# Output projection in two parts: w_out's block 3 and the second tile's channels move to the first part; the norms' factor -1/2 moves into a small step

## The chip, the core and the metric

The kernel runs on one core of a Trainium2 chip. The metric is the time of one execution in microseconds (us) of that core; three runs of the kernel before are summed up by their median. Beside them stands one profiled execution, from which every row below is taken. Engines: TensorE (PE, its weight loads PEld), VectorE (DVE), ScalarE (ACT), GpSimd (POOL), SyncE (SP, which here issues all the DMAs, in order).

## What is computed

A decoder block on 1024 tokens and 16 meta tokens of 1024 channels, in float32: a mixer of eight attention heads and a gated short convolution (512 channels each), an output projection, and an MLP with squared ReLU. The part that the change touches:

```python
def rms_norm(x, g):
    y = x * lax.rsqrt(jnp.mean(x * x, axis=-1, keepdims=True) + EPS)
    return y * g

y = concat([head_rms_norm(y_attn, ...), head_rms_norm(y_conv, ...)])   # 512 + 512 channels
h = h + y @ w_out                                                      # 1024 x 1024
hn = rms_norm(h, norm_mlp_g)
h = h + jnp.square(relu(hn @ w_ff1)) @ w_ff2
h = rms_norm(h, final_norm_g)
```

## The kernel before

**Precision.** Every large product is made of three matmuls on a high and a low part of each operand: `split` makes the high part by a cast on ScalarE and the low part by a subtraction on VectorE or, where it is told so, on POOL.

**Stages.** Projections, attention and the first part of the output projection share one long loop over (head, query tile), in which TensorE's spare time is filled from a generator (`fill`, a quota of us for each step): first with the projections, then with `out_conv`. `out_conv` (first part) multiplies the 512 convolution channels with blocks 4 to 7 of w_out (`wc`), for 8 tiles of 128 tokens and two halves of 512 columns, adds x and stores the rows in `h_scr`. The second part follows the loop: `mixed(i, ks)` multiplies tile `TOK[i]`'s attention channels (blocks 0 to 2 from `y_att`, block 3 from `y3`, which stays on the chip) with blocks `ks` of w_out (`wa`), `row_done(i)` adds the stored row, takes the norm (`rest_of`) with the gain `gmlp` to `hn`, and stores the row; `turn_rows(i)` transposes `hn` on TensorE in eight pieces, and several steps form the operands and their sums for the MLP (a form of Strassen's). TOK is 0, 4, 1, 5, 2, 3, 6, 7: the second tile is tile 4.

**Loads of the first part.** `wo_ahead` (line 612, at the end of the last q group) loads the first tile's convolution channels and blocks 4 to 7 whole into a pool of their own. `out_begin` (line 622, at the end of the last k group) frees the projections' memory, opens the pool `op` and splits these blocks. In `out_conv` each tile loads the next one's channels into one of two places `raw` of 512 columns; the tiles 1 to 3 also load blocks 0 to 2 through the same two places (`load_wo`), and tile 6 the attention channels of tile 0.

**Loads of the second part.** After the loop, lines 818 to 831, in this order: tile 4's channels, block 3 of w_out in two halves, two rows, the gain, the split of the channels, the split of block 3, the third tile's channels, the last row's store. The gain's DMA alone is not held in program order, nor are the two POOL multiplications by -1/2 behind it. Because block 3 comes last, the first two tiles run as follows:

```python
for i in range(2):
    mixed(i, range(NP - 1))        # blocks 0 to 2 of both tiles
for i in range(2):
    mixed(i, [NP - 1])             # block 3
    row_done(i)
    split_rows(i + 2)              # channels of a later tile, low part on POOL
    fetch_y(i + 3)
```

**Order.** A planner orders what is not held in program order (`pin` after the loop, `pe` inside it) by modelled times; each engine works its queue in order.

**The norm.** 1/sqrt is exp(-ln/2) with one Newton step. Before, the step gives -2 times the value (`minus_two_rstd`, and lines 844 to 846), and each gain is multiplied by -1/2 when it is loaded (`gain`, line 133): half on VectorE and half on POOL for the first norm, all on POOL for the two others.

Of the kernel before, what the change touches and what calls it, by code (L numbers as in the profile page):

```python
# [20 lines left out]
P = 128  # L21
# [20 lines left out]
def hymba_block(  # L42
# [53 lines left out]
    halfc = const.tile([P, 1], F32, name="halfc")  # L96
    nc.vector.memset(halfc, -0.5)
# [23 lines left out]
    def minus_two_rstd(ss, n, rows=P):  # L121
# [5 lines left out]
        pin(nc.vector.tensor_scalar(v, ss, 1.0 / n, EPS, op0=ALU.mult, op1=ALU.add))  # L127
        pin(nc.scalar.activation(r, r, AF.Exp, scale=-0.5))
        pin(nc.vector.scalar_tensor_tensor(out=t, in0=r, scalar=r, in1=v, op0=ALU.mult, op1=ALU.mult))
        pin(nc.vector.scalar_tensor_tensor(out=t, in0=t, scalar=-3.0, in1=r, op0=ALU.add, op1=ALU.mult))  # L130
        return t

    def gain(pool, src, tag, early=False):

        g = pool.tile([P, D], F32, name=tag, bufs=1)
        nc.sync.dma_start(g, src.broadcast_to([P, D]))
        for c in range(2):
            cs = slice(c * 512, (c + 1) * 512)
            if early and c == 0:
                nc.vector.tensor_scalar(g[:, cs], g[:, cs], -0.5, None, op0=ALU.mult)  # L140
            else:
                nc.gpsimd.tensor_tensor(out=g[:, cs], in0=g[:, cs], in1=halfc.broadcast_to([P, 512]), op=ALU.mult)
        return g
# [39 lines left out]
    gmix = gain(ep, norm_mix_g, "gmix", True)  # L183
# [26 lines left out]
    def norm(n):  # L210
# [4 lines left out]
        r = minus_two_rstd(ss, D, rows)  # L215
# [385 lines left out]
    def split_y(raw, n):  # L601
        yh = after["op"].tile([P, 4, P], F32R, name="yh", bufs=2)
        yl = after["op"].tile([P, 4, P], F32R, name="yl", bufs=2)
        split(yh[:, :n], yl[:, :n], raw, nc.gpsimd)
        return yh, yl
# [6 lines left out]
    def wo_ahead():  # L612
# [3 lines left out]
        raws = after["raws"] = [tw.tile([P, D], F32, name=f"ahead{k}") for k in range(NC)]  # L616
        y = after["y0"] = tw.tile([P, NC, P], F32, name="y0")
        nc.sync.dma_start(y, y_rows(y_conv, 0))
        for k in range(NC):
            nc.sync.dma_start(raws[k], wo[(NP + k) * P:(NP + k + 1) * P])  # L620

    def out_begin():
# [6 lines left out]
        after["wa"] = [[op.tile([P, D], F32R, name=f"wa{i}{k}") for i in range(2)] for k in range(NP - 1)]  # L629
# [3 lines left out]
        for k in range(NC):  # L633
            split(*w[k], after["raws"][k])
        after["wc"], after["y"] = w, y
# [7 lines left out]
    def out_conv():  # L643
# [4 lines left out]
        for t in range(NT):  # L648
# [4 lines left out]
            for c in range(2):  # L653
# [9 lines left out]
                if c == 0 and t + 1 < NT:  # L663
# [3 lines left out]
                elif c and 0 < t < NP:  # L667
# [129 lines left out]
    rows, ys_, yraw = {}, {0: after["y"][0]}, {}  # L797

    def fetch_y(i):
        if i < NT:  # L800
            if i == 1:
                raw = os.tile([P, (NP - 1) * P], F32, name="raw1")
            else:
                raw = after["op"].tile([P, 512], F32, name="raw", bufs=2)[:, :(NP - 1) * P]
# [3 lines left out]
    def split_rows(i):  # L808
        if i < NT:
            ys_[TOK[i]] = split_y(yraw.pop(i), NP - 1)  # L810
# [7 lines left out]
    fetch_y(1)  # L818
    w3 = [os.tile([P, D], F32R, name=f"wa{i}3") for i in range(2)]
    raw3 = [after["op"].tile([P, 512], F32, name="raw", bufs=2) for _ in range(2)]  # L820
    for c, raw in enumerate(raw3):
        dma(raw, wo[(NP - 1) * P:NP * P, c * 512:(c + 1) * 512])
    fetch_row(0)
    fetch_row(1)
    gmlp = gain(os, norm_mlp_g, "gbc")
    split_rows(1)
    for c, raw in enumerate(raw3):
        split(*(w[:, c * 512:(c + 1) * 512] for w in w3), raw)
    wa = after["wa"] + [w3]
    fetch_y(2)  # L830
    dma(*after["kept"])

    def rest_of(row, g, dst, gap=()):
# [10 lines left out]
        pin(nc.vector.tensor_scalar(v, ss, 1.0 / D, EPS, op0=ALU.mult, op1=ALU.add))  # L844
        pin(nc.vector.scalar_tensor_tensor(out=t, in0=r, scalar=r, in1=v, op0=ALU.mult, op1=ALU.mult))
        pin(nc.vector.scalar_tensor_tensor(out=t, in0=t, scalar=-3.0, in1=r, op0=ALU.add, op1=ALU.mult))
# [612 lines left out]
```

## Time and profile before

| | us |
|---|---|
| median of three runs | 1211.78 (1211.17 to 1214.83) |
| the profiled execution | 1215.61 |
| its span, first to last instruction | 1213.5 |
| TensorE busy in it | 1170.1 |
| VectorE, ScalarE, POOL busy | 729.2, 544.2, 225.8 |
| second part of the output projection, first matmul to the end of the last set | 514.4 to 580.5 |

The span is the profiled execution's own time less what lies around it; the median of the runs is 3.83 us less than the profiled execution. A stretch of the trace is read by the busy time of each engine in it; a wait is read on the engine that waits, with what released it. The granted clock of TensorE stands as a share of 2.4 GHz: 1.00 is 2.4 GHz, 0.50 is 1.2 GHz, and a value between is a mixture in time.

### The profile page before, as it was taken

To read this page: it belongs to the slowest core of one execution; us is meant where nothing else is said; L and a number is where in the kernel's file an instruction comes from. 1 tells how busy PE (TensorE), PEld (TensorE's weight loads), DVE (VectorE), ACT (ScalarE), POOL (GpSimd) and SP (SyncE) were. 2 spreads that over 40 slices of the span, in tenths; PEclk is the share of its full clock that TensorE was granted. 3 is DMA by queue.
4 is the path that set the end of the run, shared out by engine and by line. 5 is a ranking of instruction groups with operands and counts; after the bars stand their busy time and mean duration, and the time that the engine had idled before them with its cause. 6 is when DMAs were issued, how large, how long until landed. Compare 5 with 4: busy or idle time off the path is not lost.

```text
span 1213.5 us, 15649 instructions
## 1 busy us (share of the span) xinstructions
PE 1170.1 (96%) x5969; PEld 987.1 (81%) x5969; DVE 729.2 (60%) x979; ACT 544.2 (45%) x910; POOL 225.8 (19%) x223
## 2 busy tenths in 40 slices
PE   6999999999999899978899999999999999999997
PEld 6988989899988777867788888888888888888886
DVE  7632354435354655549868766666664546985686
ACT  6522334553555554536544343435353433434444
POOL 3011132222221211212533332313100000000000
PEclk9999999999999899989999999999999999999999
DMA  8348242452324564255345444353559756432561
GB/s 259 132 145 234 71 91 57 120 153 61 90 88 141 156 190 130 72 182 182 120 130 191 145 142 165 122 184 102 191 197 363 276 205 228 154 104 70 173 243 70
DMA packets 119978, 185.91 MB, mean 153 GB/s; under 512 B 9536, under 2 KB 61760, under 8 KB 119904
## 3 DMA queue, kind: packets, MB, share of 16 engines
q1 hardware_dynamic: 119904, 184.92, 47.6%
q8 instruction: 47, 0.77, 0.3%
q14 instruction: 27, 0.22, 0.1%
HBM read 126.30 MB, written 58.59 MB: 152 GB/s over the span
## 4 chain that ended last, share of the span: by engine, by line
PE 87%; DVE 5%; DMA 4%; ACT 3%; issue 2%; POOL 0%; SPq 0%; DVEq 0%; ACTq 0%; POOLq 0%
PE acc L1298 25%; PE acc L993 24%; PE mm L469 18%; PE tr L554 3%; PE mm L658 3%; PE wide L863 2%; PE S L255 1%; PE S L531 1%; PE S L532 1%; PE pv L568 1%; PE pv L569 1%; PE mm L255 1%; DMA raw<-y_conv 1%; PE ahead L993 1%; PE pv L570 1%
## 5 line engine op out<-in xcount | busy, mean ns | idle before, releaser
L1298 PE MATMUL acc<-w2h,a2l 128*128 128x512 f32 x440 | 171.2, 389 | 0.0
L1298 PE MATMUL acc<-w2l,a2h 128*128 128x512 f32 x440 | 171.2, 389 | 0.0
L1298 PE MATMUL acc<-w2h,a2h 128*128 128x512 f32 x440 | 171.2, 389 | 0.0
L469 PE MATMUL mm<-xh,wh 128*128 128x342 f32 (+3 forms) x416 | 145.0, 349 | 1.0 <-DVE vm L264 0.8
L469 PE MATMUL mm<-xh,wl 128*128 128x342 f32 (+3 forms) x416 | 144.9, 348 | 0.0
L469 PE MATMUL mm<-xl,wh 128*128 128x342 f32 (+3 forms) x416 | 144.7, 348 | 0.0
L118 ACT CAST a2h<-ar 128x1024 fp32r<-128x1024 f32 x54 | 56.9, 1053 | 147.1 <-PE acc L1298 92.5
L115 DVE TENSOR_TENSOR a2l<-ar,a2h 128x1024 fp32r<-128x1024 f32 x54 | 66.1, 1225 | 86.0 <-ACT a2h L118 85.9
L1298 PEld LDWEIGHTS acc<-w2l,a2h 128*128 128x128 f32 x440 | 82.6, 188 | 17.3
L1298 PEld LDWEIGHTS acc<-w2h,a2h 128*128 128x128 f32 x440 | 82.6, 188 | 17.1
L1298 PEld LDWEIGHTS acc<-w2h,a2l 128*128 128x128 f32 x440 | 82.6, 188 | 17.1
L469 PEld LDWEIGHTS mm<-xh,wh 128*128 128x128 f32 x416 | 78.5, 189 | 7.8 <-DVE vm L264 1.1
L469 PEld LDWEIGHTS mm<-xl,wh 128*128 128x128 f32 x416 | 78.6, 189 | 6.1
L469 PEld LDWEIGHTS mm<-xh,wl 128*128 128x128 f32 x416 | 78.5, 189 | 6.1
L115 DVE TENSOR_TENSOR ptl<-tr,pth 128x512 fp32r<-128x512 f32 (+1 forms) x96 | 56.3, 597 | 37.9 <-ACT pth L118 37.4
L115 POOL TENSOR_TENSOR wl<-wr,wh 128x512 fp32r<-128x512 f32 x40 | 53.5, 1357 | 115.9 <-ACT wh L118 103.9
L786 ACT ACTIVATE ac<-ac 128x1024 f32<-128x1024 f32 (+1 forms) x64 | 66.5, 1040 | 15.1 <-DVE ac L780 14.1
L541 ACT ACTIVATE pr<-S,nm 128x144 f32<-128x144 f32 (+3 forms) x64 | 48.5, 757 | 46.1 <-DVE nm L537 44.6
L118 ACT CAST pth<-tr 128x512 fp32r<-128x512 f32 (+1 forms) x96 | 47.9, 514 | 46.6 <-PE tr L554 34.3
L537 DVE TENSOR_REDUCE nm<-S 128x1 f32<-128x144 f32 (+3 forms) x64 | 49.4, 772 | 24.8 <-PE S L534 24.1
L780 DVE TENSOR_TENSOR ac<-acc,cv 128x512 f32<-128x512 f32 x61 | 41.7, 687 | 32.7 <-PE acc L993 32.5
L118 ACT CAST ws12h<-w1s 128x1024 fp32r<-128x1024 f32 x16 | 16.8, 1050 | 91.7 <-PE acc L993 90.0
(280 smaller groups left out, 2711.5 us busy)
## 6 DMA issues: line engine op xcount, KB each, us to landing
ar<-a_scr SPq DMA_DIRECT2D x54, 512.0 KB
w1r<-in_w_ff_dram SPq DMA_DIRECT2D x16, 1024.0 KB
a_scr<-ac SPq DMA_DIRECT2D x16, 1024.0 KB
a_scr<-sm SPq DMA_DIRECT2D x16, 768.0 KB
w<-in_w_ff_dram SPq DMA_DIRECT2D x24, 512.0 KB
wr<-in_w_in_dram SPq DMA_DIRECT2D x40, 256.0 KB
w2r<-in_w_ff_dram SPq DMA_DIRECT2D x16, 512.0 KB
k_scr<-pg SPq DMA_DIRECT2D x8, 520.0 KB
```

The costliest lines, as they stand in the source:

```text
L115: pin((eng or nc.vector).tensor_tensor(out=lo, in0=src, in1=r32(hi), op=ALU.subtract))
L118: pin(nc.scalar.copy(hi, src))
L255: pin(nc.tensor.matmul(ps[half], lhs, w_[:, k, f0:f0 + fn], start=k == 0 and a == 0, stop=k == KD - 1 and a == len(terms) - 1))
L469: pe(nc.tensor.matmul(ps, x_[:, k], y_[:, k, ts], start=k == 0 and a == 0, stop=k == KD - 1 and a == 2))
L537: nc.vector.tensor_reduce(nm, ps, axis=AX.XY, op=ALU.max, negate=True)
L541: nc.scalar.activation(pr[:, :n + pad].rearrange("p (a b) -> p a b", b=v), ps, AF.Exp, bias=nm, accum_out=s)
L554: pe(nc.tensor.transpose(ps[:, jj], pr[:, kt * P:(kt + 1) * P], ident))
L658: pe(nc.tensor.matmul(ps, y_[:, k], w_[:, cs], start=k == 0 and a == 0, stop=k == NC - 1 and a == 2))
L780: pin(eng.tensor_tensor(out=out, in0=a, in1=b, op=ALU.add))
L786: pin(nc.scalar.activation(out, src, func, **more))
L993: pe(nc.tensor.matmul(ps, w[w_][:, k], m[m_][:, k], start=k == a == 0, stop=k == HK - 1 and a == 2))
L1298: pe(nc.tensor.matmul(banks[tt], w[w_][:, k, tt * P:(tt + 1) * P], m[m_][:, k], start=first and f == k == a == 0, stop=last and f == len(f ...
```

## The change

Block 3 of w_out (`wa[3]`) is loaded in `out_conv` at tile 4, by `load_wo` as the three others, and lies in `op`. Block 7 (the last of the first part) is no longer loaded ahead but in `out_begin`, by `load_wo` through the two `raw` places. The second tile's attention channels are loaded at the last tile of `out_conv` into a place of their own (`raw1`). With both there, `mixed` runs all four blocks of each tile, and the loop over the first two tiles is one loop. The channels' low parts in the second part are made on VectorE in place of POOL. The gain's DMA is held in program order. In the norms, -1/2 goes into `v` (the mean and EPS times -1/2), and the Newton step becomes `(r*r*v + 1.5)*r`; the multiplications of the gains by -1/2 fall away. In the last norm the scaled half sum gets a third column in `ss`, one small step more for each of four tiles.

```diff
@@ -93,8 +93,6 @@
     nc.vector.memset(epsc, EPS)
-    halfc = const.tile([P, 1], F32, name="halfc")
-    nc.vector.memset(halfc, -0.5)
     onec = const.tile([P, 1], F32, name="onec")
@@ -118,28 +116,26 @@
-    def minus_two_rstd(ss, n, rows=P):
+    def newton(t, r, v):
+
+        pin(nc.vector.scalar_tensor_tensor(out=t, in0=r, scalar=r, in1=v, op0=ALU.mult, op1=ALU.mult))
+        pin(nc.vector.scalar_tensor_tensor(out=t, in0=t, scalar=1.5, in1=r, op0=ALU.add, op1=ALU.mult))
+
+    def rstd(ss, n, rows=P):
...
         pin(nc.scalar.activation(r, ss, AF.Ln, bias=epsc[:rows], scale=1.0 / n))
-        pin(nc.vector.tensor_scalar(v, ss, 1.0 / n, EPS, op0=ALU.mult, op1=ALU.add))
+        pin(nc.vector.tensor_scalar(v, ss, -0.5 / n, -0.5 * EPS, op0=ALU.mult, op1=ALU.add))
         pin(nc.scalar.activation(r, r, AF.Exp, scale=-0.5))
-        pin(nc.vector.scalar_tensor_tensor(out=t, in0=r, scalar=r, in1=v, op0=ALU.mult, op1=ALU.mult))
-        pin(nc.vector.scalar_tensor_tensor(out=t, in0=t, scalar=-3.0, in1=r, op0=ALU.add, op1=ALU.mult))
+        newton(t, r, v)
         return t
-    def gain(pool, src, tag, early=False):
+    def gain(pool, src, tag):
         g = pool.tile([P, D], F32, name=tag, bufs=1)
-        nc.sync.dma_start(g, src.broadcast_to([P, D]))
-        for c in range(2):
-            cs = slice(c * 512, (c + 1) * 512)
-            if early and c == 0:
-                nc.vector.tensor_scalar(g[:, cs], g[:, cs], -0.5, None, op0=ALU.mult)
-            else:
-                nc.gpsimd.tensor_tensor(out=g[:, cs], in0=g[:, cs], in1=halfc.broadcast_to([P, 512]), op=ALU.mult)
+        pin(nc.sync.dma_start(g, src.broadcast_to([P, D])))
         return g
@@ -180,7 +176,7 @@
     load_tokens()
-    gmix = gain(ep, norm_mix_g, "gmix", True)
+    gmix = gain(ep, norm_mix_g, "gmix")
     wvr = []
@@ -212,7 +208,7 @@
         pin(nc.scalar.activation(xn, xt, AF.Square, accum_out=ss))
-        r = minus_two_rstd(ss, D, rows)
+        r = rstd(ss, D, rows)
         for c in range(2):
@@ -598,10 +594,10 @@
-    def split_y(raw, n):
+    def split_y(raw, n, eng=nc.gpsimd):
         yh = after["op"].tile([P, 4, P], F32R, name="yh", bufs=2)
         yl = after["op"].tile([P, 4, P], F32R, name="yl", bufs=2)
-        split(yh[:, :n], yl[:, :n], raw, nc.gpsimd)
+        split(yh[:, :n], yl[:, :n], raw, eng)
         return yh, yl
@@ -613,10 +609,10 @@
         tw = ahead.enter_context(tc.tile_pool(name="tw", bufs=1, side="right", reuse_waits="tile"))
-        raws = after["raws"] = [tw.tile([P, D], F32, name=f"ahead{k}") for k in range(NC)]
+        raws = after["raws"] = [tw.tile([P, D], F32, name=f"ahead{k}") for k in range(NC - 1)]
         y = after["y0"] = tw.tile([P, NC, P], F32, name="y0")
         nc.sync.dma_start(y, y_rows(y_conv, 0))
-        for k in range(NC):
+        for k in range(NC - 1):
             nc.sync.dma_start(raws[k], wo[(NP + k) * P:(NP + k + 1) * P])
@@ -626,12 +622,13 @@
         y3["l"] = op.tile([P, T], F32R, name="y3l")
-        after["wa"] = [[op.tile([P, D], F32R, name=f"wa{i}{k}") for i in range(2)] for k in range(NP - 1)]
+        after["wa"] = [[op.tile([P, D], F32R, name=f"wa{i}{k}") for i in range(2)] for k in range(NP)]
         wc = wcpool.enter_context(tc.tile_pool(name="wc", bufs=1, reuse_waits="tile"))
...
         y = split_y(after["y0"], NC)
-        for k in range(NC):
+        for k in range(NC - 1):
             split(*w[k], after["raws"][k])
+        load_wo(NP + NC - 1, *w[NC - 1])
         after["wc"], after["y"] = w, y
@@ -660,11 +657,14 @@
                     ahead.close()
-                if c == 0 and t + 1 < NT:
+                if c == 0 and t == NT - 1:
+                    raw = after["raw1"] = after["op"].tile([P, NP - 1, P], F32, name="raw1")
+                    pe(nc.sync.dma_start(raw, y_rows(y_att, NT // 2)))
+                elif c == 0:
                     y = load_y(y_conv, t + 1, NC)
...
                     after["y"] = [load_y(y_att, 0, NP - 1)]
-                elif c and 0 < t < NP:
+                elif c and 0 < t <= NP:
                     load_wo(t - 1, *after["wa"][t - 1])
@@ -794,20 +794,17 @@
     TOK = [0, 4, 1, 5, 2, 3, 6, 7]
-    rows, ys_, yraw = {}, {0: after["y"][0]}, {}
+    rows, ys_, yraw = {}, {0: after["y"][0]}, {1: after["raw1"]}
...
         if i < NT:
-            if i == 1:
-                raw = os.tile([P, (NP - 1) * P], F32, name="raw1")
-            else:
-                raw = after["op"].tile([P, 512], F32, name="raw", bufs=2)[:, :(NP - 1) * P]
+            raw = after["op"].tile([P, 512], F32, name="raw", bufs=2)[:, :(NP - 1) * P]
             yraw[i] = raw.rearrange("p (k c) -> p k c", c=P)
...
         if i < NT:
-            ys_[TOK[i]] = split_y(yraw.pop(i), NP - 1)
+            ys_[TOK[i]] = split_y(yraw.pop(i), NP - 1, nc.vector)
@@ -815,19 +812,12 @@
-    fetch_y(1)
-    w3 = [os.tile([P, D], F32R, name=f"wa{i}3") for i in range(2)]
-    raw3 = [after["op"].tile([P, 512], F32, name="raw", bufs=2) for _ in range(2)]
-    for c, raw in enumerate(raw3):
-        dma(raw, wo[(NP - 1) * P:NP * P, c * 512:(c + 1) * 512])
     fetch_row(0)
     fetch_row(1)
+    split_rows(1)
     gmlp = gain(os, norm_mlp_g, "gbc")
-    split_rows(1)
-    for c, raw in enumerate(raw3):
-        split(*(w[:, c * 512:(c + 1) * 512] for w in w3), raw)
-    wa = after["wa"] + [w3]
     fetch_y(2)
+    wa = after["wa"]
     dma(*after["kept"])
@@ -841,24 +831,22 @@
             f()
-        pin(nc.vector.tensor_scalar(v, ss, 1.0 / D, EPS, op0=ALU.mult, op1=ALU.add))
-        pin(nc.vector.scalar_tensor_tensor(out=t, in0=r, scalar=r, in1=v, op0=ALU.mult, op1=ALU.mult))
-        pin(nc.vector.scalar_tensor_tensor(out=t, in0=t, scalar=-3.0, in1=r, op0=ALU.add, op1=ALU.mult))
+        pin(nc.vector.tensor_scalar(v, ss, -0.5 / D, -0.5 * EPS, op0=ALU.mult, op1=ALU.add))
+        newton(t, r, v)
         pin(nc.vector.scalar_tensor_tensor(out=dst, in0=row, scalar=t, in1=g, op0=ALU.mult, op1=ALU.mult))
...
-    def mixed(i, ks):
+    def mixed(i):
...
         ys = [(yh[:, k], yl[:, k]) for k in range(NP - 1)] + [(y3["h"][:, ts], y3["l"][:, ts])]
-        if i not in pss:
-            pss[i] = wide()
+        pss[i] = wide()
         for c in range(2):
             cs = slice(c * 512, (c + 1) * 512)
-            for k in ks:
+            for k in range(NP):
                 for a, (y_, w_) in enumerate(((0, 0), (0, 1), (1, 0))):
@@ -941,9 +929,7 @@
     for i in range(2):
-        mixed(i, range(NP - 1))
-    for i in range(2):
-        mixed(i, [NP - 1])
+        mixed(i)
         row_done(i)
@@ -960,7 +946,7 @@
             gap = [partial(sums_part, n, which, 1) for which in range(2)]
-        mixed(i, range(NP))
+        mixed(i)
         if i == NT - 1:
@@ -1335,6 +1321,7 @@
         pin(nc.vector.tensor_scalar(nc_[:, 1:2], nc_[:, 0:1], 1.0 / D, EPS, op0=ALU.mult, op1=ALU.add))
+        pin(nc.vector.tensor_scalar(nc_[:, 2:3], nc_[:, 1:2], -0.5, None, op0=ALU.mult))
         pin(nc.vector.tensor_tensor(out=v[tt], in0=ht[1][tt][:, hi], in1=gfin[:, hi], op=ALU.mult))
@@ -1348,9 +1335,8 @@
         yield
-        pin(nc.vector.tensor_scalar(w, s2, 1.0 / D, ss[:, 1:2], op0=ALU.mult, op1=ALU.add))
-        pin(nc.vector.scalar_tensor_tensor(out=t, in0=r, scalar=r, in1=w, op0=ALU.mult, op1=ALU.mult))
-        pin(nc.vector.scalar_tensor_tensor(out=t, in0=t, scalar=-3.0, in1=r, op0=ALU.add, op1=ALU.mult))
+        pin(nc.vector.tensor_scalar(w, s2, -0.5 / D, ss[:, 2:3], op0=ALU.mult, op1=ALU.add))
+        newton(t, r, w)
         act(o[:, hi], v[tt], AF.Copy, scale=t)
@@ -1374,7 +1360,7 @@
             add(both, v[tt].unsqueeze(1).broadcast_to([P, 2, HD2]), both)
-            ss = sst[tt] = op2.tile([P, 2], F32, name=f"ss{tt}")
+            ss = sst[tt] = op2.tile([P, 3], F32, name=f"ss{tt}")
             act(v[tt], h1[:, hi], AF.Square, accum_out=ss[:, 0:1])
```

## Rows read from the trace of the kernel before

**Rows 1.** The page, part 1: busy time, share of span, instructions.
```profile
PE 1170.1 (96%) x5969; PEld 987.1 (81%) x5969; DVE 729.2 (60%) x979; ACT 544.2 (45%) x910; POOL 225.8 (19%) x223
```

**Rows 2.** Stretches, columns as in the header row.
```profile
core 0: us, PE busy (x) PEld busy (x) DVE busy (x) ACT busy (x) POOL busy (x), PEclk, DMA share, GB/s
...
500.00:514.40 14.40, 14.40 (x88) 12.35 (x87) 7.25 (x13) 7.07 (x14) 3.36 (x3) 1.00 0.11 40
...
519.30:521.40 2.10, 0.08 (x2) 0.01 (x1) 1.82 (x2) 0.87 (x2) 2.04 (x2) 1.00 0.96 392
...
521.40:529.70 8.30, 8.30 (x28) 6.31 (x28) 1.71 (x2) 0.09 (x1) 0.00 (x0) 0.79 0.24 88
...
534.10:544.40 10.30, 9.85 (x40) 8.11 (x40) 4.87 (x7) 3.91 (x8) 1.01 (x1) 0.75 0.37 124
...
544.40:580.50 36.10, 32.50 (x153) 25.91 (x154) 32.87 (x42) 22.79 (x41) 9.90 (x7) 1.00 0.55 177
...
610.00:900.00 290.00, 290.00 (x1245) 233.46 (x1244) 198.58 (x229) 125.53 (x137) 80.69 (x56) 1.00 0.46 155
```

**Rows 3.** TensorE's timeline: start, duration, work, [idle before <- releaser].
```profile
514.41 0.71 PE L863 MATMUL wide<-wa,yh 128*128 128x512 f32 x2
...
521.39 0.50 PE L863 MATMUL wide<-wa,yl 128*128 128x512 f32 x1 [2.02 <-POOL yl L115]
...
534.07 1.94 PE L877 MATMUL wide<-ident,hn 128*128 128x128 f32 x8 [4.36 <-DVE hn L847]
...
544.48 0.70 PE L863 MATMUL wide<-wa,yh 128*128 128x512 f32 x2 [0.53 <-DVE h L780]
...
550.09 1.04 PE L877 MATMUL wide<-ident,hn 128*128 128x128 f32 x8
...
574.87 0.70 PE L863 MATMUL wide<-wa,yh 128*128 128x512 f32 x2
```

**Rows 4.** VectorE's timeline; the sixth row is line 847's summary (min/median/max).
```profile
528.35 1.23 DVE L780 TENSOR_TENSOR h<-wide,h 128x1024 f32<-128x1024 f32 x1 [6.47 <-PE wide L863]
...
531.86 2.07 DVE L847 SCALAR_TENSOR_TENSOR hn<-h,rs_t,gbc 128x1024 f32<-128x1024 f32 x1
...
551.23 0.68 DVE L115 TENSOR_TENSOR xdl<-wide,xdh 128x512 fp32r<-128x512 f32 x1
...
571.05 1.22 DVE L846 SCALAR_TENSOR_TENSOR rs_t<-rs_t,rs_r 128x1 f32<-128x1 f32 x1
...
576.95 1.28 DVE L847 SCALAR_TENSOR_TENSOR hn<-h,rs_t,gbc 128x1024 f32<-128x1024 f32 x1
...
L847 DVE SCALAR_TENSOR_TENSOR hn<-h,rs_t,gbc x8: 1284/1676/2100, 531.9 to 584.5; 128x1024 f32<-128x1024 f32 x8
```

**Rows 5.** POOL's timeline, 510 to 585.
```profile
517.45 2.49 POOL L142 TENSOR_TENSOR gbc<-gbc,halfc 128x512 f32<-128x512 f32 x2 [4.87 <-DMA gbc<-in_norm_mlp_g_dram]
...
531.86 0.99 POOL L115 TENSOR_TENSOR yl<-raw,yh 128x384 fp32r<-128x384 f32 x1 [10.52 <-ACT yh L118]
...
570.96 1.30 POOL L115 TENSOR_TENSOR w1al<-w1t,w1ah 128x512 fp32r<-128x512 f32 x1
```

**Rows 6.** SyncE's queue: start, duration, DMA.
```profile
404.13 0.54 SPq L651 DMA_DIRECT2D h<-in_x_dram  x1
...
513.33 0.33 SPq L136 DMA_DIRECT2D gbc<-in_norm_mlp_g_dram  x1
```

**Rows 7.** First part: ScalarE's timeline (one row), TensorE's (two rows).
```profile
436.27 0.62 ACT L118 CAST yh<-raw 128x512 fp32r<-128x512 f32 x1 [3.87 <-DMA raw<-y_conv]
...
413.33 0.71 PE L658 MATMUL mm<-wc,yh 128*128 128x512 f32 x2
...
436.94 0.73 PE L658 MATMUL mm<-wc,yh 128*128 128x512 f32 x2 [0.58 <-ACT yh L118]
```

**Rows 8.** VectorE's timeline at the start.
```profile
6.59 0.98 DVE L129 SCALAR_TENSOR_TENSOR rs_t<-rs_r,rs_v 128x1 f32<-128x1 f32 x1
...
13.42 0.22 DVE L129 SCALAR_TENSOR_TENSOR rs_t<-rs_r,rs_v 128x1 f32<-128x1 f32 x1 [0.41 <-ACT rs_r L128]
```

## The prediction

> **What bounds the kernel now.** I read the page's engine shares first: TensorE is busy for 1170.1 us of a span of 1213.5 us [rows 1], so all that can be won is in the 43 us in which it stands still or runs at half clock. The table of stretches says where these lie. From 610 to 900 us it stands still for 0.00 us, and in the last 14 us of the first part of the output projection also [rows 2]. The stage that the diff rewrites, 514.4 to 580.5, is different: TensorE stands still for 2.0 us of the stretch from 519.3, for 4.4 us between 529.7 and 534.1, which the table leaves out, and for 3.6 us of the long loop from 544.4, and the stretches behind the first two have a granted clock of 0.79 and 0.75, so part of them ran at 1.2 GHz [rows 2, 3]. TensorE's timeline gives the reasons [rows 3]. At 521.39 it had waited 2.02 us for POOL's low part of token tile 4 (the second tile in the order of TOK). At 534.07 it had waited 4.36 us for VectorE's normalized rows `hn` of the first tile.
>
> The first wait ends a chain: the DMA of the gain is issued at 513.33 [rows 6], those of the second tile's channels and of w_out's last block behind it, POOL multiplies the gain from 517.45 to 519.94 first, and only then subtracts for `yl` [rows 5]. The second wait is one of order: because w_out's block 3 comes late, tile 0 gets blocks 0 to 2, tile 1 gets blocks 0 to 2, then tile 0 gets block 3. So tile 0's sum is ready one block before tile 1's, and its norm (add at 528.35, `hn` begun at 531.86 and 2.07 us long [rows 4]) has only six matmuls to hide under.
>
> **The change part by part.** *Order of the first two tiles.* Block 3 of w_out and tile 4's channels now come in the first part, so `mixed(0)` and `mixed(1)` run whole, 24 matmuls each. From 544.48 to 550.09 such a set takes 5.6 us at 2.4 GHz, and the eight transposes behind it 1.04 us [rows 3]; I take 1.1 with the hand-over. Starting at 514.4 as now: tile 0 to 520.0, tile 1 to 525.6. Tile 0's norm takes 3.51 us from the start of the add to the start of `hn`, plus 1.28 us for an undisturbed `hn` (the one of 576.95) [rows 4]: ready at 520.0 + 4.8 = 524.8, under tile 1. So the transposes run 525.6 to 526.7, tile 2 to 532.3, the next transposes to 533.4. Tile 3 needs a PSUM place that the add of tile 2 frees: 532.3 + 1.23 [rows 4] + 0.15 = 533.7. Before, that set began at 544.48 [rows 3]. **Gain 10.8 us.** It contains 2.0 and 4.4 us of waits; the other 4.4 us is the half clock after each (28 matmul records in the 8.3 us behind the first wait, 40 in the 10.3 us behind the second, at 0.79 and 0.75 [rows 2]). It supposes that no such wait comes back. Tile 4's channels need the places of `yh`, `yl` that the last convolution tile frees at 513.3, then a cast (0.62 us for 512 columns [rows 7], fewer here) and VectorE's 0.55 (below): about 514.5, wanted at 520. The gain, wanted at 523.5, may be issued anywhere from 513.33 (its place in this profile) to about 519 and still lands in its 4 us. It is now pinned behind the two row loads and ahead of tile 1's channels and the last row store; all of these are wanted later than 523.
>
> *POOL's subtraction of the channels goes to VectorE, and the gain's multiplications go.* From 544.4 to 580.5 VectorE is the bound: 32.87 of 36.1 us busy [rows 2]. On it the move costs, per tile, 384 columns, by the line through 512 columns in 0.68 us and 1024 in 1.23 us [rows 4]: 0.55 us, four times in that stretch, 2.2 us. It gives back what POOL held up: `hn` took 2.07 us with POOL's `yl` beginning at the same 531.86, and 1.28 us without [rows 4, 5]. Half of the eight `hn` are slow ones (least 1.284, median 1.676, most 2.100 [rows 4]); of the four tiles of that stretch two lost 0.8 us so, one 0.6 us and one 1.7 us in 128x1 steps (the longest took 1.22 us beside POOL's w1 subtraction of 570.96 [rows 4, 5]): 3.9 us. Net 1.7 us won on VectorE. POOL keeps the low parts of w1 (1.30 us for the one of 570.96 [rows 5]), two of which would now meet VectorE's new subtraction: 0 to 2.6 us. So the four intervals after tile 3, 30.4 us now (544.48 to 574.87 [rows 3]), change by -2.5 (also the shorter stalls that hang on VectorE) to +0.9. I take **-1.0**, as POOL's operation is ready while `hn` holds VectorE, and one of the two is likely to pass between `hn` and the subtraction.
>
> First the row, then the rule on this: when both began at 531.86, POOL's took its normal 0.99 us and VectorE's waited [rows 4, 5]. The Trainium skill, "SBUF — State Buffer", section "SBUF: two separate sides", says that whichever of a GpSimd operation and a VectorE operation with two SBUF inputs starts first holds the shared ports for its whole length. By that rule the moved subtraction, with two SBUF inputs, stays exposed to every GpSimd operation left; with both w1 subtractions in front the sum would be +0.9 in this place and not -1.0. The trace agrees as far as the pairs of [rows 4, 5] go.
>
> *The first part pays.* (a) Block 7 of w_out, until now a 512 KB load issued long before, becomes two halves through the two `raw` places in `out_begin`, and its casts and subtractions wait for them in the queues of ScalarE and VectorE, with the softmax's exponentials behind. TensorE wants this block at 413.33 [rows 7], for the tenth matmul of the first set, 9 us after the first load into the same pool was issued (404.13 [rows 6]). (b) The second convolution tile's channels use the same two places and come some 5 us later than now. (c) The last block for the second part adds two loads, two casts of 0.62 [rows 7] and two subtractions of 0.68 [rows 4] at tile 4. What such a load can do to ScalarE's queue is shown at 436.27: 3.87 us of waiting, of which 0.58 us reached TensorE at 436.94 [rows 7]. Bounds: -0.5 (ScalarE has a cast less in front of an exponential) to +4.0 (one whole such wait reaching TensorE); the nearest row is that of 436.94, 0.6 us and nearly as much again for a slow clock behind it, so **+1.0**. (d) Tile 4's channels have a place of their own and wait for nobody: 0, covered by 6 us of DMA at 0.11 load [rows 2].
>
> *Start.* The first `rs_t` step took 0.98 us beside POOL's multiplication of gmix [rows 8]; the one of 13.42 took 0.22 [rows 8]. TensorE's first transpose waits for this, and it has little idle time after. Bounds 0 (a later load of x may be what counts) to -0.8: **-0.6**.
>
> *Nothing.* The factor -1/2 moves into `v` with as many instructions as before; the four 128x1 steps added in `last_gain` run while TensorE still has 48 matmuls queued, and if that cover were gone they would cost four such steps, 0.9 us. The gain of the last norm loses two POOL multiplications in a stage that TensorE bounds. On SP's queue 0.7 MB less stands behind 513.33, which costs nothing there.
>
> **Sum**: -10.8 - 1.0 + 1.0 - 0.6 = -11.4 us. The profiled execution took 1215.61 us around a span of 1213.5; it should become 1204.2 around 1202.1. The median of the three runs shown is 3.83 us below the profiled one, so the same sum on it gives 1211.78 - 11.4 = **1200.4 us**. Behind 604 us both halves of the MLP are bound by TensorE, so nothing there should swallow the gain.
>
> **The rivals.** *The lock takes the place of the wait.* Both w1 subtractions pass in front of VectorE and the delay reaches TensorE's next set; the half clock comes back once. For it: VectorE is 91% busy there. Against: both are short. Price: +1.9 against my -1.0 and some 2 us of half clock, so 1204.5 us.
>
> *The late block.* One whole wait of the kind of 436.27 reaches TensorE in the first part, and the half clock costs as much again for a part of it. For it: [rows 7]. Against: block 7 is wanted 9 us after it can be issued. 1200.4 - 1.0 + 6 = 1205.4 us.
>
> *The change doesn't do what it says.* The planner puts the second tile's cast, or the last attention norm's, behind something late, so that tile 1 still waits and tile 0's norm is bared again: only the 2.0 us wait or the like is won, minus the cost of the first part: about 1210 us.
>
> *Slower.* In `out_begin` the cast of block 7 stands in ScalarE's queue in front of the exponentials, and its load is held by SP's queue, where loads wait for stores of k. Every microsecond that it lands after 410 costs TensorE one, and nearly one again at half clock. It decides the sign from a landing about 8 us late: 16 us lost against 11.4 + 1.0 won, 1216 us. Nothing in the trace waits that long for a load in this stage (3.87 us is the longest).
>
> **How the numbers follow.** Forecast as worked out 0.62; the lock 0.10; the late block 0.13; not what it says 0.09; slower 0.06. Ends of the first: -14 (second part -13.3, start -0.8, first part 0) gives 1197.5; the two next cases end at 1206. I take 1197 to 1207, which leaves out the last two cases and some of the first's edge. A measurement of this kernel can tell 0.3% from no change, 3.6 us: faster below 1208.1, slower above 1215.4. Faster 0.85, same 0.09, slower 0.06.
>
> **What would show it.** Right: in the timeline after the change 24 matmuls of tile 0 and 24 of tile 1 without a gap, the first transposes of `hn` 11 us behind the first matmul, clock 1.00 up to the loop; `hn` at 1.28 us in all tiles; the loop's last set about 12 us earlier against the first. Wrong: a wait of TensorE for `yl`, `y3` or the gain in that place; a wait of more than 2 us of ScalarE for `raw` between 400 and 420; more idle time of TensorE from 400 to 514 than before. The forecast falls altogether if the gain is found in that stage and lost again ahead of 514.

## The result and the profile after

The kernel after takes 1192.49 us (median of four runs, 1191.37 to 1195.17) beside 1212.66 us for the kernel before on the same chip: a ratio of 0.9836, 95% interval [0.9812, 0.9859]. That is 20.2 us won where 11.4 were forecast, and a time below the range of 1197 to 1207. The profiled execution took 1195.17 us around a span of 1193.4.

Where the time went shows when the profiled executions are cut at the same points of the work (the start of the first matmul of each stage in TensorE's timeline, us from the span's start):

| from | to | before | after | change | forecast |
|---|---|---|---|---|---|
| span's start | first transpose | 8.69 | 7.50 | -1.2 | -0.6 |
| first transpose | `mixed(0)` | 505.7 | 506.3 | +0.6 | +1.0 |
| `mixed(0)` | `mixed(3)` | 30.07 | 18.94 | -11.1 | -10.8 |
| `mixed(3)` | `mixed(7)` | 30.39 | 30.54 | +0.15 | -1.0 |
| `mixed(7)` | MLP's first half | 29.20 | 29.10 | -0.1 | 0 |
| MLP's first half, 1272 matmuls | | 296.79 | 288.33 | **-8.5** | 0 |
| MLP's second half and the end | | 312.67 | 312.61 | -0.1 | 0 |

The page's first part, as in [rows 1]:

```profile
PE 1155.6 (97%) x5969; PEld 982.8 (82%) x5969; DVE 727.7 (61%) x989; ACT 544.5 (46%) x911; POOL 212.5 (18%) x211
```

TensorE issues the same 5969 matmuls and is busy for 14.5 us less. Stalls that go would not lower this number; half clock that goes would, and so would matmuls that have become shorter. Both happened. First the stage that was forecast; the table of stretches, cut like [rows 2]:

```profile
core 0: us, PE busy (x) PEld busy (x) DVE busy (x) ACT busy (x) POOL busy (x), PEclk, DMA share, GB/s
...
514.00:525.00 11.00, 11.00 (x51) 9.05 (x51) 5.42 (x9) 4.32 (x9) 0.00 (x0) 1.00 0.58 189
525.00:533.00 8.00, 7.47 (x42) 6.22 (x40) 5.11 (x8) 4.21 (x8) 0.00 (x0) 1.00 0.53 172
533.00:563.30 30.30, 26.37 (x128) 21.11 (x128) 28.55 (x41) 18.60 (x35) 3.20 (x2) 1.00 0.57 184
```

Where [rows 2] had stretches at a granted clock of 0.79 and 0.75, the clock is 1.00 throughout. TensorE's timeline (start, duration, work, idle time before and what ended it), the rows that answer to [rows 3]:

```profile
513.84 0.71 PE L851 MATMUL wide<-wa,yh 128*128 128x512 f32 x2
...
524.84 1.03 PE L865 MATMUL wide<-ident,hn 128*128 128x128 f32 x8
...
532.78 0.70 PE L851 MATMUL wide<-wa,yh 128*128 128x512 f32 x2 [0.53 <-DVE h L780]
...
563.32 0.70 PE L851 MATMUL wide<-wa,yh 128*128 128x512 f32 x2 [0.54 <-DVE h L780]
```

The 48 matmuls of the first two tiles run from 513.84 to 524.84 without a gap; the waits of 2.02 and 4.36 us are gone. Then the MLP's first half, which was forecast to stay as it is. One form of matmul from the stretch 610 to 875 us of either kernel (count, busy time in us, mean duration in ns, idle time before), before and then after:

```profile
L993 PE MATMUL acc<-xah,wf0h 128*128 128x512 f32 x96 | 38.0, 396 | 0.0
```
```profile
L979 PE MATMUL acc<-xah,wf0h 128*128 128x512 f32 x104 | 40.5, 389 | 0.0
```

The same instruction on the same shape at the same clock takes 396 ns before and 389 after (a record runs from the start to the modelled end, so it overlaps its neighbours). From start to start it is 296.79 / 1272 = 233.3 ns before and 288.33 / 1272 = 226.7 ns after, as a mean over that half; the records of all its forms show the same step. TensorE never stands still there in either kernel. In the second half a matmul takes 389 ns in both kernels. So the 8.5 us that the forecast lacks are not a stall that went: the 1272 matmuls follow each other 6.6 ns sooner.

### The profile page after: what moved, and what is told of

It is laid out like the page before. It is cut to its first block, busy times and chain, and to the rows that moved or that the text cites. A ratio compares the mean times of both kernels' runs of the same rounds, so it can differ in the third digit from the quotient of the medians.

```text
span 1193.4 us, 15645 instructions
## 1 busy us (share of the span) xinstructions
PE 1155.6 (97%) x5969; PEld 982.8 (82%) x5969; DVE 727.7 (61%) x989; ACT 544.5 (46%) x911; POOL 212.5 (18%) x211
## 4 chain that ended last, share of the span: by engine, by line
PE 87%; DVE 5%; DMA 3%; ACT 3%; issue 2%; DVEq 0%; ACTq 0%; SPq 0%
PE acc L1284 26%; PE acc L979 24%; PE mm L465 18%; PE tr L550 3%; PE mm L655 2%; PE wide L851 2%; PE mm L251 2%; PE S L251 1%; PE pv L564 1%; PE pv L565 1%; PE S L527 1%; PE S L528 1%; DMA raw<-y_conv 1%; DMA raw<-in_w_out_dram 1%; PE pv L566 1%
```

## The experiments

**What made the matmuls of the MLP's first half shorter?** The diff touches no line of that stage except the last gain's multiplications. It does remove a constant of 128x1. That tile took 32 bytes in each partition, and it stood among the first tiles on one side of SBUF, so everything behind it moved down by 32 bytes, the MLP's weights among it; the moving operands xa to xd lie on the other side and stayed. The built programs give the places: in the kernel before, the moving operands of that half start at 480 modulo 512 and its weights at 0; after, both at 480. The first three kernels add 32 unused bytes, on one side or the other, and the fourth adds them on both.

e1, and e2 in the same way on the kernel before:

```
+    nc.vector.memset(const.tile([P, 1], F32, name="pad0"), 0.0)
     onec = const.tile([P, 1], F32, name="onec")
```

> The kernel after with one unused 128x1 tile put back among the constants, where the removed -1/2 stood: every tile behind it on that side of SBUF moves up by 32 bytes, nothing else changes. In the first half of the MLP the moving operands (xa to xd, on the other side) then start at 32 bytes past a multiple of 64 and the weights at a multiple of 64, as in the kernel before; after, both started at 32 past. Theories: (1) the weights' start alone sets the pace: matmuls of that half at 233.5 ns from start to start again instead of 226.7, 1272 of them, the half 8.5 us longer (296.8 us), about 1201 us. (2) The difference of the two starts sets it: the same, 1201 us. (3) The 8.5 us came from less work on POOL and VectorE or from another order: nothing moves, 1192.5 us.

> The kernel before with one more unused 128x1 tile among the constants: everything behind it on that side moves up by 32 bytes, all its work and order stay. (1) and (2): the first half of the MLP goes from 296.8 to 288.3 us, matmuls from 233.5 to 226.7 ns, the whole 1204 us. (3), the place has nothing to do with it: 1212.7 us.

e3, and e4 together with the line of e1:

```
     bx = xs.enter_context(tc.tile_pool(name="bx", bufs=1, side="right", reuse_waits="tile"))
+    nc.vector.memset(bx.tile([P, 8], F32, name="bxlow"), 0.0)
...
     xd = pair(bx, [P, HK, HT], "xd")
+    nc.vector.memset(bx.tile([P, 8], F32, name="bxtop"), 0.0)
```

> The kernel after with 32 unused bytes on either side of xa to xd, so that the moving operands of the MLP's first half start at a multiple of 64, and the weights stay at 32 past one. (1) weights alone: 226.7 ns stays, 1192.5 us. (2) the difference of the starts: 233.5 ns, 1201 us. (3): 1192.5 us.

> The two shifts together: moving operands and weights of the MLP's first half both start at a multiple of 64. (1) weights alone: 233.5 ns, 1201 us. (2) the difference of the starts: 226.7 ns, 1192.5 us. (3): 1192.5 us.

Measured against the kernel before: e1 0.9906 [0.9888, 0.9925], e2 1.0002 [0.9989, 1.0016], e3 0.9912 [0.9891, 0.9933], e4 0.9918 [0.9891, 0.9945]. The first half took 296.80, 296.80, 296.79 and 296.80 us. The stretch from 620 to 860 us lies wholly inside that half; in it TensorE is busy for all of the 240 us, and the count of matmuls tells their pace (a row gives TensorE's busy time, its matmuls, the granted clock, the DMA share and GB/s). First e1, then e2:

```profile
620.00:860.00 240.00, 240.00 (x1030) 1.00 0.45 153
```
```profile
620.00:860.00 240.00, 240.00 (x1030) 1.00 0.48 157
```

What follows: one unused tile costs 8.5 us (0.9906 against 0.9836), so the place does it, and theory (3), less work or another order, falls. But (1) and (2) fall too, in the form they had: in e3 the weights lie as after and it is slow all the same, and in e2 and e4 the two starts agree modulo 64 and it is slow. Left was a difference of the two starts modulo more than 64. For that the weights of this half alone were moved, by unused bytes at the head of their pool: 32 columns (128 bytes) in e6, 64 in e7, and 120 in e5, together with the two lines of e3:

```
     wr1 = mlp.enter_context(tc.tile_pool(name="wr1", bufs=1, reuse_waits="tile"))
+    nc.vector.memset(wr1.tile([P, 32], F32, name="wrpad"), 0.0)
```

> The kernel after with the moving operands xa to xd 32 bytes lower (as in e3_after_moving32) and, in the MLP alone, the weights 480 bytes higher (unused bytes ahead of them): the two starts, which agree modulo 512 after, agree modulo 512 again at another place (448 in the place of 480). (1) The difference of the two starts modulo some power of two sets the pace: 226.7 ns from start to start in the first half of the MLP, which takes 288.3 us, total 1192.5 us. (2) Only one place is fast, 480 modulo 512 for the weights or for both: about 233 ns, 296.8 us, 1201 us.

> The kernel after with 128 unused bytes ahead of the weights in the first half of the MLP: the two starts then differ by 128 modulo 512. The period of the effect is open: if it is 32, 64 or 128, 226.7 ns and 288.3 us; if it is 256 or 512, about 233 ns and 296.8 us. Differences of 32 and 64 were slow, so 128, 256 and 512 are left.

> The same with 256 bytes. Period 128 or 256: 226.7 ns and 288.3 us; period 512: about 233 ns and 296.8 us.

They took 1193.38, 1204.04 and 1192.78 us (one run each), and the first half 288.33, 295.60 and 288.32 us. The stretch of e7:

```profile
620.00:860.00 240.00, 240.00 (x1060) 1.00 0.48 158
```

All placements side by side (starts modulo 512 in bytes, difference weights minus moving modulo 256, start to start as the half's time over 1272):

| kernel | moving | weights | difference | first half, us | ns |
|---|---|---|---|---|---|
| before | 480 | 0 | 32 | 296.79 | 233.3 |
| e1 | 480 | 0 | 32 | 296.80 | 233.3 |
| e3 | 448 | 480 | 32 | 296.79 | 233.3 |
| e2 | 480 | 32 | 64 | 296.80 | 233.3 |
| e4 | 448 | 0 | 64 | 296.80 | 233.3 |
| e6 | 480 | 96 | 128 | 295.60 | 232.4 |
| after | 480 | 480 | 0 | 288.33 | 226.7 |
| e5 | 448 | 448 | 0 | 288.33 | 226.7 |
| e7 | 480 | 224 | 0 | 288.32 | 226.7 |

In this half, where all operands of a side keep one start modulo 256, the pace goes by whether the two starts agree modulo 256 and by nothing else that was varied: not by the place itself (e5), not by the change's work (before and e1). Why the distance counts, no run shows. e5 holds a control of its own: the 72 matmuls computed ahead of this half (into `ahead`) use the same moving tiles with weights of another pool, which e5 leaves 32 bytes off; they take 234 ns there (median) and 227 after.

**How much of the rest is the norm factor, how much the order?** e9 is the kernel before with the norm factors alone (hunks on `newton`, `rstd`, `gain` and the last norm), e10 the kernel after without them. In each a tile in the constant's place, an unused one in e9, keeps the places of the kernel before. The edit of e9, which e10 has the other way round:

```
-    halfc = const.tile([P, 1], F32, name="halfc")
-    nc.vector.memset(halfc, -0.5)
+    nc.vector.memset(const.tile([P, 1], F32, name="pad"), 0.0)
...
-            if early and c == 0:
-                nc.vector.tensor_scalar(g[:, cs], g[:, cs], -0.5, None, op0=ALU.mult)
-            else:
-                nc.gpsimd.tensor_tensor(out=g[:, cs], in0=g[:, cs], in1=halfc.broadcast_to([P, 512]), op=ALU.mult)
```

> The kernel before with the second half of the change alone: -1/2 goes into the norm's factors, the three gains are no longer multiplied on POOL (nor gmix's first half on VectorE). An unused 128x1 tile takes the place of the removed constant, so no tile moves. The order of the first two tiles stays that of before. (1) As the forecast has it, POOL's multiplication of gbc (2.49 us) held the low part that TensorE waits for, but the second wait of that stage is one of order: the first transpose comes 1.2 us earlier, the wait of 2.02 us and the half clock behind it (about 2 us) go, the wait of 4.36 us for the norm stays: from mixed(0) to mixed(3) 26 us in the place of 30.1 (28.4 in the run with the tiles moved), total about 1208 us. (2) The multiplication was what delayed the whole stage: 19 to 21 us from mixed(0) to mixed(3), total about 1201 us. (3) It had no part in the stage: 28.4 to 30.1 us, and the total changes by the 1.2 us of the start alone, 1211 us.

> The kernel after with the norm factors, the constant and the multiplications of the gains as before: what is left of the change is the order of the first two tiles, the loads in the first part and the low parts on VectorE. The constant stands where it stood, so the weights of the MLP's first half lie as in the kernel before (and as in e1_after_left32, 1201.2 us). (1) The order makes the gain: mixed(0) to mixed(3) stays at 18.9 us, the MLP's first half at 296.8, the first transpose comes 1.2 us later than after, total 1202 to 1203 us. (2) POOL's multiplication of gbc still reaches the norm of the first tile: 1 to 4 us more between mixed(0) and mixed(3), 1204 to 1206 us.

e9: 0.9957 [0.9945, 0.9970], 1207.59 us; `mixed(0)` to `mixed(3)` 26.36 us. e10: 0.9922 [0.9904, 0.9940], 1202.18 us; 18.89 us, first transpose at 8.75. Theory (1) has both. TensorE's timeline of e9 shows which wait goes and which stays:

```profile
510.59 0.71 PE L859 MATMUL wide<-wa,yh 128*128 128x512 f32 x2
...
515.97 0.50 PE L859 MATMUL wide<-wa,yl 128*128 128x512 f32 x1 [0.35 <-POOL yl L114]
...
526.20 1.94 PE L873 MATMUL wide<-ident,hn 128*128 128x128 f32 x8 [3.52 <-DVE hn L843]
```

Without POOL's multiplication the first wait shrinks from 2.02 us to 0.35. The second is one of order and stays, 3.52 us, with a granted clock of 0.72 in the stretch behind it. The rest of the change, without the norm factors, removes both: with the multiplication back on POOL (e10), nobody on TensorE's path waits for it, and tile 3 begins 18.89 us behind tile 0. TensorE's timeline of e10:

```profile
511.00 0.71 PE L856 MATMUL wide<-wa,yh 128*128 128x512 f32 x2
...
529.89 0.70 PE L856 MATMUL wide<-wa,yh 128*128 128x512 f32 x2 [0.54 <-DVE h L784]
```

e10 keeps the new order, the earlier loads, the low parts on VectorE and the gain's DMA in program order together, so which of these took away the wait for `yl` is not shown. In the new order the norm factor is worth the earlier start, 1.3 us (8.75 against 7.50), and, by the tile that it makes needless, the 8.5 us of the places.

**Was the move of the channels' low parts to VectorE worth anything?**

```
-            ys_[TOK[i]] = split_y(yraw.pop(i), NP - 1, nc.vector)
+            ys_[TOK[i]] = split_y(yraw.pop(i), NP - 1, nc.gpsimd if i > 1 else nc.vector)
```

> The kernel after with the low parts of the channels of the third to eighth token tile on POOL again, as before; the second tile's stays on VectorE, the rest of the change and all places in SBUF stay. From the start of mixed(3) to that of mixed(7) it was 30.4 us before and 30.5 us after. (1) As forecast, the move to VectorE won 1.0 us in this stretch and something else took it: 31.5 us, total +1.0 us. (2) The move won nothing, VectorE pays for the subtraction what POOL's waits had cost it: 30.3 to 30.7 us, total as after. (3) The move costs, because of the collisions with POOL's subtractions for w1: 29.5 us or less, total -1 us.

1191.47 us, 0.9823 [0.9796, 0.9849] against 0.9836 for after: no difference that can be measured. `mixed(3)` to `mixed(7)` took 30.34 us, inside what theory (2) said. The sum over the loop fits this: VectorE is busy there for 28.76 us before, 28.79 after and 28.73 in e8. Columns as in [rows 2], in this order:

```profile
544.48:574.87 30.39, 26.87 (x128) 21.29 (x129) 28.76 (x37) 18.84 (x35) 7.55 (x6) 1.00 0.57 184
532.78:563.32 30.54, 26.59 (x129) 21.35 (x129) 28.79 (x41) 18.84 (x35) 3.20 (x2) 1.00 0.57 183
530.23:560.57 30.34, 26.69 (x129) 21.28 (x129) 28.73 (x37) 18.83 (x35) 7.55 (x6) 1.00 0.57 184
```

What the move gives back, others take. VectorE's timeline of the kernel after, and POOL's of the same stretch:

```profile
549.23 1.28 DVE L836 SCALAR_TENSOR_TENSOR hn<-h,rs_t,gbc 128x1024 f32<-128x1024 f32 x1
550.43 1.65 DVE L113 TENSOR_TENSOR yl<-raw,yh 128x384 fp32r<-128x384 f32 x1
...
559.34 2.23 DVE L836 SCALAR_TENSOR_TENSOR hn<-h,rs_t,gbc 128x1024 f32<-128x1024 f32 x1
561.49 0.55 DVE L113 TENSOR_TENSOR yl<-raw,yh 128x384 fp32r<-128x384 f32 x1
```
```profile
549.75 1.91 POOL L113 TENSOR_TENSOR w1al<-w1t,w1ah 128x512 fp32r<-128x512 f32 x1 [37.70 <-ACT w1ah L116]
559.20 1.29 POOL L113 TENSOR_TENSOR w1al<-w1t,w1ah 128x512 fp32r<-128x512 f32 x1 [7.54 <-ACT w1ah L116]
```

Both of POOL's subtractions for w1 meet VectorE now: the first makes the moved subtraction 1.65 us long (0.55 undisturbed), the second makes `hn` 2.23 (1.28 undisturbed), 2.05 us together.

**Can the rule of the places be used elsewhere?** The q, k and convolution projections run at 233 ns for 512 columns too; there the moving operand steps by 4160 bytes from k to k+1, 64 more than a multiple of 256, and the weights by 512. Two kernels changed places alone:

```
-        wh = rp.tile([P, KD, P], F32R, name="wh", bufs=2)                # e11, wl in the same way
+        wh = rp.tile([P, KD, P + 16], F32R, name="wh", bufs=2)[:, :, :P]
...
-    xh = rp.tile([P, KD, L], F32R, name="xh")                            # e12, xl in the same way
+    xh = rp.tile([P, KD, L + 48], F32R, name="xh")[:, :, :L]
...
     lf = rp.tile([P, NK, NH], F32, name="lf")                            # both
+    nc.vector.memset(rp.tile([P, 8], F32, name="rppad"), 0.0)
```

> The kernel after with the weights of the q, k and convolution projections placed so that, in the 384 matmuls with 512 moving columns (the q groups and the third convolution groups, 8 groups of 48), moving operand and weights start at the same address modulo 256 for every k: 16 unused columns behind each 128 of the weights and 32 unused bytes ahead. If the rule found in the MLP holds there, these matmuls go from about 233 ns to 226.7, 384 x 6.5 ns = 2.5 us of TensorE's time, total 1190 us. If their 233 ns come from something else (other engines at SBUF, the interleaving with attention), nothing moves: 1192.5 us. If the rule holds but that stage waits for other engines anyway, 227 ns show and the total stays.

> As e11_after_projection_places, with the steps from k to k+1 multiples of 256 too: 48 unused columns behind each 1040 of xh and xl (the step becomes 4352 bytes = 17 x 256), the weights' step 512 as after. In e11 a moving operand and the weights loaded for the next matmul still differed by 64 at each change of k, one matmul in three. (1) What counts is the moving operand against the weights loaded while it streams: now equal in all 384 matmuls of 512 columns, 226.7 ns, 2.5 us of TensorE's time, total about 1190 us. (2) The rule of the MLP does not hold in this stage, where matmuls of the projection and of attention alternate and other engines work at SBUF: 232 ns as in e11, total 1192.5 to 1193 us.

e11: 1193.22 us, 0.9846 [0.9831, 0.9862]; the median from start to start hardly moves, 232 ns for 233 after. e12: 1192.66 us, 0.9824 [0.9800, 0.9847]; the median is 227 ns. Of the pairs of neighbouring 512-column matmuls there, 6% are at 228 ns or less after, 16% in e11, 55% in e12. The same lines of after and of e12:

```profile
L465 PE MATMUL mm<-xh,wl 128*128 128x512 f32 x128 | 51.7, 404 | 0.0
L465 PE MATMUL mm<-xl,wh 128*128 128x512 f32 x128 | 51.3, 401 | 0.0
```
```profile
L466 PE MATMUL mm<-xh,wl 128*128 128x512 f32 x128 | 51.2, 400 | 0.0
L466 PE MATMUL mm<-xl,wh 128*128 128x512 f32 x128 | 51.0, 398 | 0.0
```

So the places count in this stage too. Which weights have to agree with the moving operand stays open. One reading is that they are those loaded while it streams, the next matmul's: in e11 each matmul's own two operands agreed, and only at the change of k did the next weights differ, by 64; making the steps multiples of 256 as well gave the 227 ns. The pairs of e11 speak against this reading as it stands: by the built program's places the next weights agree too in 233 of them, and their median is 232 ns all the same, beside 233 ns for the 120 at a change of k. And e12 changed the steps of the moving operand too, so that its starts are all alike modulo 256, as they are in the MLP and are not in e11. The yield is small: the mean over these pairs fell from 241.0 to 237.6 ns, 3.4 ns x 384 = 1.3 us, as the stage is interleaved with attention, and the whole kernel's gain over after can't be told from none. No kernel here measurably beats the kernel after.

## Why the prediction was wrong, point by point

*The order of the first two tiles: right.* 18.94 us from `mixed(0)` to `mixed(3)` against 19.3 worked out, and the size is right: -11.1 for -10.8. e10 shows that it needs nothing of the norm factors. The half clock behind each wait, which the forecast had as 4.4 us, belongs to it: e9, which loses most of one wait and keeps the other, still shows 0.72 behind the one that it keeps. One reservation: in e2, the kernel before with its tiles moved by 32 bytes, the stretch takes 28.42 us in the place of 30.07. The two waits are there (2.10 and 4.36 us), but behind the first the granted clock is 1.00 (from 519.88 to 526.20), where [rows 2] has 0.79. So the half clock behind that wait, some 1.7 us of the 11.1, does not come with every execution.

*VectorE and POOL's loop: the term was mis-sized.* Forecast -1.0, measured +0.15 (and +0.20 against e8). The 2.2 us paid and the 3.9 us given back fit what is seen: the undisturbed subtraction takes 0.55 us, three of the four `hn` take 1.28, and no 128x1 step is longer than 0.22. Of the collisions with POOL's subtractions for w1 the forecast counted some 0.7 us of its bound of 2.6 ("one of the two is likely to pass between"); both met VectorE, for 2.05 us. That is the mechanism of the rival named the lock, without its half clock. The rule of the Trainium skill that was weighed there ("SBUF — State Buffer", section "SBUF: two separate sides") gave +0.9 for this place and came nearer than the forecast: POOL's operation of 559.20 began first and `hn` waited.

*The first part: the sign is right, the size can't be told closely.* +0.6 for +1.0. The cast of the second tile's channels waited, as feared under (b), and a wait of TensorE came of it. ScalarE's, VectorE's and TensorE's timelines of the kernel after (in the first, block 7's second half and then the channels):

```profile
408.16 0.62 ACT L116 CAST wc<-raw 128x512 fp32r<-128x512 f32 x1 [0.57 <-DMA raw<-in_w_out_dram]
...
411.98 0.62 ACT L116 CAST yh<-raw 128x512 fp32r<-128x512 f32 x1 [2.83 <-DMA raw<-y_conv]
```
```profile
413.12 1.02 DVE L113 TENSOR_TENSOR ptl<-tr,pth 128x512 fp32r<-128x512 f32 x2 [3.30 <-ACT pth L116]
```
```profile
416.18 0.87 PE L550 MATMUL tr<-ident,pr 128*128 128x128 f32 x6 [1.26 <-ACT pr L537]
```

ScalarE casts `pth` only behind that cast, VectorE's `ptl` waits for `pth`, and the maximum that the next softmax on ScalarE (`pr`) needs stands behind `ptl` in VectorE's queue; TensorE waits for `pr`. All eleven profiled kernels with the new first part have this wait, 2.10 to 3.73 us on ScalarE and 0.90 to 2.38 us on TensorE; none of the three with the old one has it. Block 7 itself was late by 0.57 us only. The price is less sure: the stretch from the first convolution matmul to `mixed(0)` took 107.1 us in the mean of the three (105.6 to 108.7) and 107.7 in the mean of the eleven (105.2 to 112.7), +0.6 in a spread of 7 us, and TensorE stands still in it for 4.8 us in the mean of the three (4.3 to 5.7) and for 5.9 in that of the eleven (4.6 to 7.6). Two signs that the prediction had named for being wrong came with this: a wait of ScalarE for `raw` of more than 2 us between 400 and 420, and more idle time of TensorE from 400 to 514 (8.45 us before, 9.85 after). They stayed within the price of this term and are not what made the forecast miss.

*The start: right, too small.* -1.2 for -0.6. The forecast took the 0.76 us of the one `rs_t` step. What it left out is VectorE's own multiplication of gmix, which stands ahead of that step and waits for the gain's DMA. VectorE's timeline of e10, where it is back, and the row of after that answers to [rows 8]:

```profile
6.29 0.43 DVE L140 TENSOR_SCALAR gmix<-gmix 128x512 f32<-128x512 f32 x1 [0.60 <-DMA gmix<-in_norm_mix_g_dram]
6.63 0.99 DVE L129 SCALAR_TENSOR_TENSOR rs_t<-rs_r,rs_v 128x1 f32<-128x1 f32 x1
```
```profile
6.16 0.22 DVE L121 SCALAR_TENSOR_TENSOR rs_t<-rs_r,rs_v 128x1 f32<-128x1 f32 x1 [0.41 <-ACT rs_r L131]
```

The step begins 0.47 us earlier and is 0.77 us shorter. In the profiled execution of the kernel before this wait was covered, because the first rows of x landed some 0.5 us later there (ScalarE's square began at 4.84, in e10 at 4.35): one execution can hide a wait that the next one shows.

*"Behind 604 us both halves of the MLP are bound by TensorE, so nothing there should swallow the gain": the step that failed,* together with "Nothing", whose terms left the MLP at 0. The MLP's first half was put at no change and measured -8.5 us. Both steps go from "busy for 100%" to "as short as it can be". A TensorE that never stands still can be slow all the same, and [rows 2] held the sign of it: 1245 matmuls in 290 us are 232.9 ns each, while the second half, whose matmuls have the same shape and the same clock, shows 1060 in 240 us, 226.4 ns, in the same table of the kernel before:

```profile
920.00:1160.00 240.00, 240.00 (x1060) 1.00 0.58 197
```

In the kernel before the same contrast stood once more in the stage under study: in the second part the matmuls on `y3h` and `y3l` take 235 and 233 ns (median) beside 227 for those on `yl`, and there too one block of w_out lay on the other side of SBUF, 32 bytes off modulo 256; after, with that block in `op` and 0 bytes off, they take 227. The forecast counted instructions, and a constant taken away counts as one memset less; that it is also 32 bytes less, which move every tile behind it, was in no term. It is worth 8.5 of the 8.8 us by which the forecast was short. That the rest came out so close is luck: the other terms missed by -0.3 (order), -0.6 (start), -0.4 (first part) and +1.15 us (loop), which nearly cancel. With the tile put back the whole change takes 1201.17 us (e1), beside 1200.4 forecast. (The low end of the range, -13.3 - 0.8, adds up to 1197.7 and not 1197.5; it changes nothing.)

*The rivals.* None came as a whole. The lock came by its mechanism, both subtractions meeting VectorE, but without the half clock and at a lower price. The late block came in part: 1.26 us of the 2.83 reached TensorE in the kernel after, at most 2.38 of 3.73 in another with the same first part (e6). The slower one asked for block 7 about 8 us late; it was 0.57.

## What to carry to other kernels

Before calling a stage bound by TensorE, compare its time from start to start with that of other matmuls of the same shape in the same trace: here 6.6 ns on each of 1272 matmuls were worth 8.5 us, more than the two waits of 2.02 and 4.36 us together. For such matmuls, lay out moving operands and weights so that their starts agree modulo 256 bytes (e5, e7), and their steps too (e12), and look at the places again after every edit that adds or removes a tile, however small. And when work moves from POOL to VectorE, count on VectorE its own time and also the POOL operations that it can now meet (here both did): VectorE's busy time over the whole loop (28.76, 28.79, 28.73 us) tells in one number whether anything was won.

## What the runs showed of the hardware

In the MLP's first half an fp32r matmul of 128x128 weights and 512 moving columns takes 226.7 ns from start to start at a granted clock of 1.00 if the two operands' starts agree modulo 256 bytes (after, e5, e7), and 232.4 to 233.3 ns if they are 32, 64 or 128 bytes apart (before, e1 to e4, e6; other distances weren't tried there). The weight loads keep their duration, 188 ns in both kernels; it is the matmul's record that grows from 389 to between 394 and 396 ns. In the projections, where the moving starts of e11 change from k to k+1, agreement of each matmul's own two operands was not enough (232 ns); with the steps multiples of 256 as well (e12) the median was 227.
